# Three-branch attention with two heads' score and value products side by side, and one compressed-branch step for four heads

## The chip, the cores and the metric

The kernel runs on one core of one Trainium2 chip. The metric is the device time of one execution in microseconds (us), from three runs. The engines of the core work beside each other, each through its own queue in order: TensorE (products and transposes, which write PSUM), VectorE, ScalarE, GpSimd (POOL) and SyncE, which here issues DMAs.

## What is computed

Three blocks of a small transformer on 256 tokens of width 1024: retention with a mixture of experts, a three-branch attention with a mixture of experts, and a block of a state space model with a dilated attention and a feed-forward part. The change touches only the three-branch attention (the reference's `nsa_shared_kv` and `nsa_attention`): 16 query heads in 4 groups of 4, each group sharing its keys and values, head width 64. Each head attends to compressed keys (15 of them, pooled from windows of 32 tokens), to selected blocks, and to a window; the three results are weighted by gates and added. With 256 tokens every block of 64 is selected and every earlier token lies in the window, so both of these are causal attentions with different keys and values.

```python
        s = jnp.einsum('bgrqd,bgnd->bgrqn', qb, k_cmp).astype(jnp.float32)
        p_cmp = masked_softmax(s, cmp_end[None, :] <= t[:, None])
        o_cmp = jnp.einsum('bgrqn,bgnd->bgrqd', p_cmp.astype(dt), v_cmp)
...
        s = jnp.einsum('bgrqd,bgqkd->bgrqk', qb, ks).astype(jnp.float32)
        p = masked_softmax(s, (key_pos <= t[:, None])[:, :, None])
        o_slc = jnp.einsum('bgrqk,bgqkd->bgrqd', p.astype(dt), vs)
...
        s = jnp.einsum('bgrqd,bgkd->bgrqk', qb, kw).astype(jnp.float32)
        p = masked_softmax(s, wmask)
        o_win = jnp.einsum('bgrqk,bgkd->bgrqd', p.astype(dt), vw)
        o = gb[..., 0:1] * o_cmp + gb[..., 1:2] * o_slc + gb[..., 2:3] * o_win
```

## The kernel before

The whole network is one program; a planner (`schedule_with_timeline_sim=True`) orders each engine's instructions from the program text, its dependencies and its own estimate of times, so the order on an engine is not that of the text. `tc.issue_after(x)` holds the instructions inside it behind x in that order.

Products of full precision weights are made of three products of split operands (`mm3`, L237 to L241: L239, L240, L241); the split itself is a cast on ScalarE (L228) and a subtraction on VectorE (L230). Plain float32 products appear in the trace as two MATMUL records each, transposes as one.

The three-branch attention is `nsa` (from L955). It makes keys and values, then the compressed ones (L1077 to L1097): `kcz` holds compressed keys, `vcm` [16, 4, 64] compressed values with the 15 positions on partitions. `proj(I["w_q"], ...)` with `rope` makes the queries in two halves (L1100 to L1108), each of 8 heads: `qT` has two heads of 64 features on the 128 partitions. The first half serves groups 0 and 1.

Then come 8 steps over 4 groups g and 2 token tiles tb of 128 tokens. `scores(g, tb)` (L1113) makes, for the two head pairs pr of the group, the compressed scores of the pair (L1123, mask L1124), and for each head sl of the pair the scores over selected and window keys together (L1129; 64 partitions are contracted, [128, 2, S] results, S = 128 or 256 keys), then the causal mask, added by a bfloat16 product with the identity (L1130), the row maximum on VectorE (L1132) and two exponentials on ScalarE that also add up the denominators (L1134). The compressed scores have a maximum on VectorE (L1125) and an exponential per head (L1137). Denominators and gates make the factor `sc` (L1140 to L1142), and VectorE scales the probabilities (L1147); GpSimd scales the compressed ones (L1143).

`values(g, tb)` transposes the probabilities (L1161), copied from PSUM by VectorE and ScalarE in turn (L1163, L1165), and the compressed probabilities of the four heads, 16 columns each (L1169, L1171); then it adds all value products of a head half in one PSUM tile `po` (L1180): head half sl = 0 writes partitions 0 to 63, sl = 1 partitions 64 to 127. The result is split for the next projection (L234, L235). `scores` of the next step is asked for ahead of `values` of this one.

PSUM tiles of one bank come from three rings: `pmm` (4 banks: projections, scores and, here, compressed scores), `pat` (2: value results), `ptr` (2: transposes). The output projection (`w_no`, L1195 to L1198) takes all four banks of `pmm`; the planner runs its products between the last values. `ln_route` and the experts (`moe`) follow.

Of the kernel before, what the change touches and what calls it, by code (L numbers as in the profile page):

```python
# [20 lines left out]
EPS = 1e-5  # L21
# [4 lines left out]
OFFSET = 2.0 ** 20  # what tells the tokens of an expert from the others in their ranks  # L26
# [4 lines left out]
# where the first weights of a layer's experts go, in their order, and the order of loading where it is another one  # L31
# [4 lines left out]
# ---------------------------------------------------------------- host layout  # L36
# [137 lines left out]
# ---------------------------------------------------------------- kernel body  # L174
class Prog:
# [30 lines left out]
    # PSUM tiles of one bank  # L206
# [36 lines left out]
    def unit_a(self, outs, src, aT, k0, nk):  # L243
        """tokens on partitions: outs[t] [128, 512] += aT^T . unit (4 k tiles from k0 of nk)"""
# [10 lines left out]
    def ends_a(self, units, pool=()):  # L255
        """the last units of a projection, (outs, src, aT, k0, nk, tile of aT at k0): one token tile after the other;
        pool: what GpSimd's share of the splits comes after"""
# [15 lines left out]
    def unit_b(self, out, src, aT, k0, nk, engs=(None, None)):  # L273
        """features on partitions: out [128, 2, 256] += unit^T . aT (8 k tiles from k0 of nk)"""
# [8 lines left out]
    def unit_a256(self, outs, src, aT):  # L283
        """tokens on partitions: outs[t] [128, 256] = aT^T . unit (8 k tiles)"""
# [10 lines left out]
    def router(self, l, pool, room, tags, bufs):  # L295
        """the router's weights with the gain of the norm before it, and what its shift adds to the scores"""
# [16 lines left out]
    def route(self, t, pool):  # L313
        """the experts of token tile t: two of the best of four groups; the lower index first where equal"""
# [11 lines left out]
        # a group's score: the sum of its two best  # L326
# [8 lines left out]
        # how many of its group come before each one  # L335
# [12 lines left out]
        # the rank of each token within its expert, in order: OFFSET + rank where the expert is the token's  # L348
# [10 lines left out]
    def onehot(self, qd, t, r, pool):  # L359
        """which token of tile t has which slot of the experts 4 qd to 4 qd + 3 (r: the ranks)"""  # L360
# [7 lines left out]
    def ln_route(self, po, gb, hT, router, pool):  # L368
        """h = LN(alpha h + po), and each token's experts; hT [128, 2, 8, 128] is room"""
# [60 lines left out]
    def rstd(self, out, var):  # L430
        """out = (var + EPS) ** -0.5"""
# [6 lines left out]
    def ln_rows(self, i, gb):  # L438
        """gain and shift of norm i on all partitions, [128, 2, 1024]"""
        src = self.I["ln_r"][i]  # L440
        self.nc.gpsimd.dma_start(gb, bass.AP(tensor=src.tensor, offset=src.offset, ap=[[0, 128], [1024, 2], [1, 1024]]))
        return gb
# [1225 lines left out]
```

## Time and profile before

| what | value |
|---|---|
| median of 3 runs | 1499.23 us (1496.37 to 1500.24) |
| span of the profiled execution | 1498.9 us |
| TensorE busy | 1427.4 us, 95% of the span |
| VectorE busy | 776.1 us, 52% |
| ScalarE busy | 555.0 us, 37% |
| granted TensorE clock, mean | 0.978 of full speed |

The windows view gives for a stretch (from:to in us) its length and then the busy us of PE (TensorE products), PEld (its weight loads), DVE (VectorE), ACT (ScalarE) and POOL (GpSimd), each with its instruction count, then the granted clock, the DMA engines' busy share and GB/s. A timeline row gives start, busy us, engine, line, operation, written tile<-read tiles, for TensorE the rows*columns of the array in use and the moving shape, and the count of merged instructions; idle time before it stands in brackets. A group row gives line, engine, operation, tiles, shapes and count, then busy us and mean ns of one, then the engine's idle time before them and what ended it. Busy times of matmuls that follow one another overlap, so the distance between two starts tells what one costs.

### The profile page before, as it was taken

Reading aid. Unit: us, or ns where it says so; the run is one execution under the profiler, and the core shown is the slowest. Engines: PE = TensorE matmul, PEld = TensorE weight load, DVE = VectorE, ACT = ScalarE, POOL = GpSimd, SP = SyncE. Lnnn points to the kernel's source line nnn. Section 1 sums busy time; section 2 is a strip of 40 time slices with the busy share of each in tenths; the row PEclk is TensorE's granted clock in tenths of the full one; section 3 lists DMA queues with packets and bytes.
Section 4 is the critical chain, followed back from the end, with each engine's and each line's share of the span. In section 5 each row is a group of like instructions: output and inputs, shape, how many; then the busy total and the mean of one; then the engine's idle time right before and its main releaser. Section 6 shows DMA issues by size and latency. Waiting matters only on the chain. (4 is left out here: it accounts for less than half of the span.)

```text
span 1498.9 us, 20993 instructions
## 1 busy us (share of the span) xinstructions
PE 1427.4 (95%) x8363; PEld 1016.1 (68%) x8363; DVE 776.1 (52%) x1229; ACT 555.0 (37%) x978; POOL 232.8 (16%) x206
## 2 busy tenths in 40 slices
PE   7999988998998999989998999999999999899997
PEld 6888764443444875564443444997999999699986
DVE  5655563221215456553221215598999775745445
ACT  3434421110112555611110112566878554344442
POOL 2222121000002420021000001002443320211111
PEclk9999998999999999998998999999999999999999
DMA  9845677999984473166999984553765435545550
GB/s 359 330 155 169 257 279 280 375 417 389 414 351 166 160 273 145 57 255 263 362 419 389 414 319 177 198 207 112 265 211 196 156 127 171 194 144 194 187 179 28
DMA packets 64489, 365.16 MB, mean 244 GB/s; under 512 B 7472, under 2 KB 13120, under 8 KB 27648
## 3 DMA queue, kind: packets, MB, share of 16 engines
q1 hardware_dynamic: 60576, 348.75, 62.0%
q0 software_dynamic: 3808, 15.00, 2.8%
q8 instruction: 68, 1.11, 0.3%
q14 instruction: 37, 0.30, 0.1%
HBM read 362.53 MB, written 1.18 MB: 243 GB/s over the span
## 5 line engine op out<-in xcount | busy, mean ns | idle before, releaser
L230 DVE TENSOR_TENSOR wlo<-raw,whi 128x1024 fp32r<-128x1024 f32 x239 | 297.8, 1251 | 230.3 <-ACT whi L228 229.8
L228 ACT CAST whi<-raw 128x1024 fp32r<-128x1024 f32 x254 | 265.0, 1048 | 308.0 <-PE mm L241 129.9
L797 PE MATMUL mm<-raw,xg 128*64 128x512 f32 x744 | 187.2, 618 | 0.0
L241 PE MATMUL mm<-th,wlo 128*128 128x256 f32 x544 | 154.9, 285 | 4.3 <-DVE wlo L230 4.3
L239 PE MATMUL mm<-th,whi 128*128 128x256 f32 x544 | 155.9, 287 | 0.0
L240 PE MATMUL mm<-tl,whi 128*128 128x256 f32 x544 | 154.8, 285 | 0.0
L797 PEld LDWEIGHTS mm<-raw,xg 128*64 128x64 f32 x744 | 56.5, 141 | 93.2 <-issue 88.7
L241 PEld LDWEIGHTS mm<-th,wlo 128*128 128x128 f32 x544 | 104.2, 192 | 5.7 <-DVE wlo L230 4.7
L239 PEld LDWEIGHTS mm<-th,whi 128*128 128x128 f32 x544 | 104.3, 192 | 2.3 <-issue 1.2
L240 PEld LDWEIGHTS mm<-tl,whi 128*128 128x128 f32 x544 | 104.3, 192 | 1.3 <-issue 1.1
L235 DVE TENSOR_TENSOR y<-mm,y 128x512 fp32r<-128x512 f32 x32 | 22.0, 692 | 143.5 <-ACT y L234 142.3
L230 POOL TENSOR_TENSOR wlo<-raw,whi 128x1024 fp32r<-128x1024 f32 x15 | 37.5, 2505 | 305.7 <-ACT whi L228 305.7
L817 PE MATMUL mm<-raw,wk 128*64 128x512 f32 x344 | 80.5, 596 | 0.9 <-ACT wk L810 0.9
L240 PE MATMUL at<-tl,whi 128*128 128x256 f32 x264 | 74.8, 284 | 0.2 <-DVE tl L235 0.2
L239 PE MATMUL at<-th,whi 128*128 128x256 f32 x264 | 74.7, 283 | 0.2 <-ACT th L234 0.2
L241 PE MATMUL at<-th,wlo 128*128 128x256 f32 x264 | 74.7, 283 | 0.0
L234 ACT CAST y<-mm 128x512 fp32r<-128x512 f32 x32 | 18.7, 586 | 121.0 <-PE mm L817 120.8
L817 PEld LDWEIGHTS mm<-raw,wk 128*64 128x64 f32 x344 | 25.7, 137 | 45.7 <-issue 42.7
L850 DVE TENSOR_TENSOR h<-h,at 128x512 f32<-128x512 f32 x48 | 31.7, 685 | 46.4 <-PE at L844 45.0
L241 PE MATMUL mm<-whi,xl 128*128 128x512 f32 x128 | 51.2, 400 | 0.0
L240 PEld LDWEIGHTS at<-tl,whi 128*128 128x128 f32 x264 | 50.7, 192 | 0.7 <-DVE tl L235 0.4
L239 PEld LDWEIGHTS at<-th,whi 128*128 128x128 f32 x264 | 50.6, 192 | 0.7 <-ACT th L234 0.5
(448 smaller groups left out, 3152.9 us busy)
## 6 DMA issues: line engine op xcount, KB each, us to landing
raw<-in_w_moe SPq DMA_DIRECT2D x136, 1024.0 KB, 9.9
raw<-in_w_in SPq DMA_DIRECT2D x37, 1024.0 KB, 4.9
raw<-in_w_ret SPq DMA_DIRECT2D x31, 1024.0 KB, 5.0
wlo<-in_w_moe SPq DMA_DIRECT2D x40, 512.0 KB, 10.0
whi<-in_w_moe SPq DMA_DIRECT2D x40, 512.0 KB, 9.5
raw<-in_w_up SPq DMA_DIRECT2D x16, 1024.0 KB, 4.8
raw<-in_w_dn SPq DMA_DIRECT2D x16, 1024.0 KB, 4.9
hT<-in_w_moe SPq DMA_DIRECT2D x8, 1024.0 KB, 11.3
```

The source lines that it names most:

```text
L228: self.nc.scalar.copy(hi, src)
L230: (eng or self.nc.vector).tensor_sub(lo, src, hi.bitcast(F32))
L234: self.nc.scalar.copy(hi, src)
L235: self.last = self.nc.vector.tensor_sub(lo, src, hi.bitcast(F32))
L239: mm(out, lh, rh, start=start, stop=False)
L240: mm(out, lh, rl, start=False, stop=False)
L241: return mm(out, ll, rh, start=False, stop=stop)
L797: P.last_gu = nc.tensor.matmul(p[e * 64:(e + 1) * 64], xg[:, k, s0 + e * 64:s0 + e * 64 + 64], r[e][:, k2], start=k == 0, stop=k == 7)
L817: nc.tensor.matmul(pd[j][e * 64:(e + 1) * 64], hT_[:, k, e * 64:(e + 1) * 64], r[e][:, j], start=k == 0, stop=k == 3)
L850: V.tensor_add(h[:, t, c], h[:, t, c], p)
```

## The change

Scores: the compressed scores of all four heads of the group now come first, in a tile of the `pat` ring; one maximum, one subtraction, one exponential and one sum treat four heads at once, in two fixed tiles `Pcs` of 4 x 32 columns. For each head pair the two heads' score products are issued one behind the other, on partitions 0 to 63 and 64 to 127, into two banks, and both masks come after them. The first of a pair waits for the last exponential of the pair before last (`done[-2]`).

Values: the products of both head halves alternate. The compressed probabilities of four heads are transposed at once (128 columns); the compressed values `vcz` [128, 4, 4, 64] are kept once for each head position on 32 partitions of their own, with zeros elsewhere, so that a head's product runs over 128 rows and 128 moving columns. `hv` is the hidden layer spread out to 4 x 32 columns to make them.

Order: the second half of the queries is made after the first scores. The rest of the diff takes comments out of the text. Its core:

```diff
-        vcm = small.tile([16, 4, 64], F32, name="vcm", bufs=1)
+        vcz = small.tile([128, 4, 4, 64], F32, name="vcz", bufs=1)
+        Pcs = [small.tile([128, 4, 32], F32, name=f"Pc{i}", bufs=1) for i in range(2)]
...
-            G.memset(vcm, 0.0)
+            G.memset(vcz, 0.0)
+            for Pc in Pcs:
+                G.memset(Pc, 0.0)
...
-        p = P.pat([16, 4, 64])
+        hv = early.tile([128, 2, 4, 4, 32], F32, name="hv")
+        G.memset(hv, 0.0)
+        for hb in range(2):
+            V.tensor_copy(hv[:, hb, :, :, 0:15], hidT[:, hb, 1, :, None, 0:15].to_broadcast([128, 4, 4, 15]))
+        p = P.pat([128, 4, 64])
         for g in range(4):
             for hb in range(2):
-                mm(p[0:15, g], hidT[:, hb, 1, g, 0:15], wc2[:, 1, hb, 0:64], start=hb == 0, stop=hb == 1)
-        V.tensor_copy(vcm[0:15], p[0:15])
+                mm(p[:, g], hv[:, hb, g].rearrange("p r n -> p (r n)"), wc2[:, 1, hb, 0:64], start=hb == 0, stop=hb == 1)
+        for r in range(4):
+            V.tensor_copy(vcz[32 * r:32 * r + 32, r], p[32 * r:32 * r + 32])
         router = P.router(1, rp, early, ("rw", "lnp"), 1)
-        for c in range(2):
+        def queries(c):
...
-        heads.close()
-        oh = hT_pool.tile([128, 8, 256], F32R, tag="Th", name="oh")
-        ol = hT_pool.tile([128, 8, 256], F32R, tag="Tl", name="ol")
+        done = []
         def scores(g, tb):
             S = 128 * (tb + 1)
             ts = slice(tb * 128, tb * 128 + 128)
-            nm = small.tile([128, 2, 3, 2], F32, tag="nm", name="nm", bufs=2)
+            nm = small.tile([128, 2, 2, 2], F32, tag="nm", name="nm", bufs=2)
+            nmc = small.tile([128, 4], F32, tag="nmc", name="nmc", bufs=2)
             den = small.tile([128, 2, 3, 2], F32, tag="den", name="den", bufs=2)
             Pt = room(f"P{tb}", [128, 2, 2, 2, S])
-            Pc = small.tile([128, 2, 2, 16], F32, tag="Pc", name="Pc", bufs=2)
-            pc = P.pmm([128, 2, 2, 16])
+            Pc = Pcs[tb]
+            pc = P.pat([128, 2, 2, 16])
             for pr in range(2):
                 q = qT[:, 2 * g + pr, ts]
                 mm(pc[:, pr], q, kcz[:, g], start=True, stop=False)
                 mm(pc[:, pr], P.identb, cmb[:, tb, None, :].to_broadcast([128, 2, 16]), start=False, stop=True)
-                V.tensor_reduce(nm[:, pr, 0], pc[:, pr], axis=AX.X, op=ALU.max, negate=True)
+            pch = pc.rearrange("p a s n -> p (a s) n")
+            V.tensor_reduce(nmc, pch, axis=AX.X, op=ALU.max)
+            V.tensor_tensor(Pc[:, :, 0:16], pch, nmc[:, :, None].to_broadcast([128, 4, 16]), op=ALU.subtract)
+            A.activation(Pc[:, :, 0:16], Pc[:, :, 0:16], AF.Exp)
+            V.tensor_reduce(den[:, :, 0], Pc[:, :, 0:16].rearrange("p (a s) n -> p a s n", a=2), axis=AX.X, op=ALU.add)
+            for pr in range(2):
+                q = qT[:, 2 * g + pr, ts]
+                ps = [P.pmm([128, 2, 256]) for _ in range(2)]
+                pair = []
                 for sl in range(2):
                     c = slice(64 * sl, 64 * sl + 64)
-                    ps = P.pmm([128, 2, 256])
-                    mm(ps[:, :, 0:S], q[c], kz[c, g, :, 0:S], start=True, stop=False)
-                    mm(ps[:, :, ts], P.identb, P.causalb[:, None, :].to_broadcast([128, 2, 128]),
-                       start=False, stop=True)
-                    V.tensor_reduce(nm[:, pr, 1:3, sl], ps[:, :, 0:S], axis=AX.X, op=ALU.max, negate=True)
+                    with tc.issue_after(pair[0].ins) if pair else nullcontext():
+                        pair.append(mm(ps[sl][:, :, 0:S], q[c], kz[c, g, :, 0:S], start=True, stop=False))
+                if len(done) > 1:
+                    tc.add_manual_dep(pair[0].ins, done[-2].ins.name, mybir.DependencyInfo(
+                        mybir.DependencyClass.Sync, mybir.DependencyReason.ANTI), reason="both of a pair")
+                with tc.issue_after(pair[1].ins):
+                    for sl in range(2):
+                        mm(ps[sl][:, :, ts], P.identb, P.causalb[:, None, :].to_broadcast([128, 2, 128]),
+                           start=False, stop=True)
+                for sl in range(2):
+                    V.tensor_reduce(nm[:, pr, :, sl], ps[sl][:, :, 0:S], axis=AX.X, op=ALU.max, negate=True)
                     for br in range(2):
-                        A.activation(Pt[:, pr, br, sl], ps[:, br, 0:S], AF.Exp,
-                                     bias=nm[:, pr, 1 + br, sl:sl + 1], accum_out=den[:, pr, 1 + br, sl:sl + 1])
-                for sl in range(2):
-                    A.activation(Pc[:, pr, sl], pc[:, pr, sl], AF.Exp, bias=nm[:, pr, 0, sl:sl + 1],
-                                 accum_out=den[:, pr, 0, sl:sl + 1])
+                        last = A.activation(Pt[:, pr, br, sl], ps[sl][:, br, 0:S], AF.Exp,
+                                            bias=nm[:, pr, br, sl:sl + 1], accum_out=den[:, pr, 1 + br, sl:sl + 1])
+                done.append(last)
             sc = small.tile([128, 2, 3, 2], F32, tag="sc", name="sc", bufs=2)
             V.reciprocal(sc.rearrange("p a b c -> p (a b c)"), den.rearrange("p a b c -> p (a b c)"))
             V.tensor_mul(sc, sc, gat[:, tb, 12 * g:12 * g + 12].rearrange("p (a s b) -> p a b s", a=2, s=2))
             V.tensor_scalar(sc[:, :, 0], sc[:, :, 0], cmpc[:, 32 + tb:33 + tb], None, op0=ALU.mult)
-            G.tensor_tensor(Pc, Pc, sc[:, :, 0, :, None].to_broadcast([128, 2, 2, 16]), op=ALU.mult)
+            Pca = Pc[:, :, 0:16].rearrange("p (a s) n -> p a s n", a=2)
+            G.tensor_tensor(Pca, Pca, sc[:, :, 0, :, None].to_broadcast([128, 2, 2, 16]), op=ALU.mult)
...
-            p = P.ptr([16, 2, 2, 128])
-            for sl in range(2):
-                for pr in range(2):
-                    nc.tensor.transpose(p[:, sl, pr], Pc[:, pr, sl], P.ident)
-            PTc = rp.tile([16, 2, 2, 128], F32, tag="S", name="PTc", bufs=1)
+            p = P.ptr([128, 128])
+            nc.tensor.transpose(p, Pc.rearrange("p r n -> p (r n)"), P.ident)
+            PTc = rp.tile([128, 128], F32, tag="S", name="PTc", bufs=1)
             A.copy(PTc, p)
             po = P.pat([128, 2, 128])
-            jobs = []
-            for br in range(2):
-                for sb in range(nb):
-                    jobs.append((vv[:, sb, br, g], lambda sl, br=br, sb=sb: PT[:, sl, br, sb]))
-            jobs.append((vcm[:, g], lambda sl: PTc[:, sl]))
-            for sl in range(2):
-                for n, (lh, rh) in enumerate(jobs):
-                    mm(po[sl * 64:(sl + 1) * 64], lh, rh(sl), start=n == 0, stop=n == len(jobs) - 1)
+            for n, (br, sb) in enumerate((br, sb) for br in range(2) for sb in range(nb)):
+                for sl in range(2):
+                    mm(po[sl * 64:(sl + 1) * 64], vv[:, sb, br, g], PT[:, sl, br, sb], start=n == 0, stop=False)
+            for pr in range(2):
+                for sl in range(2):
+                    mm(po[sl * 64:(sl + 1) * 64, pr], vcz[:, 2 * pr + sl, g], PTc, start=False, stop=pr == 1)
             P.hilo(oh[:, 2 * g:2 * g + 2, ts], ol[:, 2 * g:2 * g + 2, ts], po)
 
         order = [(g, tb) for g in range(4) for tb in range(2)]
-        ahead = None
+        queries(0)
+        ahead = scores(0, 0)
+        queries(1)
+        heads.close()
+        oh = hT_pool.tile([128, 8, 256], F32R, tag="Th", name="oh")
+        ol = hT_pool.tile([128, 8, 256], F32R, tag="Tl", name="ol")
...
```

## Rows read from the trace of the kernel before

**Rows 1.** The profile's page: busy us, share of the span and instructions by engine.
```profile
PE 1427.4 (95%) x8363; PEld 1016.1 (68%) x8363; DVE 776.1 (52%) x1229; ACT 555.0 (37%) x978; POOL 232.8 (16%) x206
```

**Rows 2.** Windows view, the attention stretch: busy us by engine, clock, DMA, GB/s.
```profile
629.00:663.00 34.00, 34.00 (x157) 23.93 (x155) 15.62 (x31) 9.22 (x17) 1.46 (x3) 1.00 0.50 178
553.00:663.00 110.00, 109.43 (x509) 62.00 (x507) 61.76 (x175) 57.02 (x229) 7.61 (x14) 1.00 0.36 135
```

**Rows 3.** TensorE's timeline, scores of token tile 1: start, us, line, shapes, records.
```profile
576.24 1.12 PE L1129 MATMUL mm<-kz,qT 64*128 64x512 f32 x2
577.29 0.28 PE L1130 MATMUL mm<-causalb,identb 128*128 128x256 bf16 x1
577.50 1.12 PE L1129 MATMUL mm<-kz,qT 64*128 64x512 f32 x2
578.56 0.28 PE L1130 MATMUL mm<-causalb,identb 128*128 128x256 bf16 x1
578.68 0.60 PE L1161 MATMUL tr<-com,P 128*128 128x128 f32 x4
579.21 1.08 PE L1180 MATMUL at<-Q,vv 128*64 128x256 f32 x4
```

**Rows 4.** TensorE's timeline, scores of token tile 0.
```profile
588.67 0.70 PE L1129 MATMUL mm<-kz,qT 64*128 64x256 f32 x2
589.29 0.28 PE L1130 MATMUL mm<-causalb,identb 128*128 128x256 bf16 x1
589.51 0.70 PE L1129 MATMUL mm<-kz,qT 64*128 64x256 f32 x2
```

**Rows 5.** TensorE's timeline, value products and transposes of the compressed branch.
```profile
583.46 0.64 PE L1180 MATMUL at<-PTc,vcm 16*64 16x256 f32 x2
584.03 1.94 PE L1180 MATMUL at<-Q,vv 128*64 128x256 f32 x8
...
587.13 0.60 PE L1169 MATMUL tr<-com,Pc 128*16 128x128 f32 x4
587.66 1.08 PE L1180 MATMUL at<-Q,vv 128*64 128x256 f32 x4
```

**Rows 6.** TensorE's timeline, value products of the later dilated attention.
```profile
1021.16 1.95 PE L1248 MATMUL at<-dPT,v 128*64 128x256 f32 x16
```

**Rows 7.** VectorE's groups, 553 to 663: count, busy us, mean ns, idle before.
```profile
L1132 DVE TENSOR_REDUCE nm<-mm 128x2 f32<-128x512 f32 x16 | 11.0, 690 | 8.4 <-PE mm L1130 8.3
L1147 DVE TENSOR_SCALAR P<-P,sc 128x256 f32<-128x256 f32 x32 | 9.1, 355 | 0.0
...
L1147 DVE TENSOR_SCALAR P<-P,sc 128x128 f32<-128x128 f32 x32 | 6.8, 282 | 0.0
L1132 DVE TENSOR_REDUCE nm<-mm 128x2 f32<-128x256 f32 x16 | 6.6, 422 | 6.3 <-PE mm L1130 6.2
...
L1125 DVE TENSOR_REDUCE nm<-mm 128x2 f32<-128x32 f32 x16 | 2.9, 184 | 6.1 <-PE mm L1124 6.0
```

**Rows 8.** ScalarE's groups, 553 to 663.
```profile
L1134 ACT ACTIVATE P<-mm,nm 128x256 f32<-128x256 f32 x32 | 14.8, 471 | 8.7 <-PE tr L1161 5.6 <-DVE nm L1132 3.0
...
L1137 ACT ACTIVATE Pc<-mm,nm 128x16 f32<-128x16 f32 x32 | 8.3, 267 | 1.0 <-DVE nm L1125 1.0
```

**Rows 9.** Windows view of the later state space stage.
```profile
1050.00:1162.00 112.00, 109.30 (x958) 103.54 (x955) 103.84 (x162) 86.95 (x201) 43.82 (x33) 1.00 0.65 222
```

**Rows 10.** Timeline where the compressed keys and values are made.
```profile
536.58 0.55 PE L1089 MATMUL at<-hidT,wc 128*128 128x64 f32 x4
...
537.06 1.07 PE L1096 MATMUL at<-wc,hidT 128*15 128x64 f32 x16
...
538.92 0.74 POOL L1008 TENSOR_TENSOR qr<-rope,rope 128x256 f32<-128x256 f32 x1 [20.08 <-DVE rope L1000]
```

**Rows 11.** Windows view of the stretch behind the attention.
```profile
680.00:690.00 10.00, 8.69 (x33) 4.21 (x33) 4.67 (x20) 0.53 (x2) 2.39 (x3) 0.63 0.21 11
690.00:700.00 10.00, 10.00 (x54) 4.92 (x54) 1.38 (x2) 1.87 (x2) 0.00 (x0) 1.00 0.92 379
```

## Prediction

> **What bounds the kernel now.** I read the profile from the outside in. The page first: TensorE is busy 95% of the span, and no other engine is above 52%, PEld aside [rows 1]. That is an average over very different stages, so next comes the windows view of the stretch that the change touches, from the first score product of the attention (553 us) to the last product of its output projection (663 us): TensorE is busy 109.4 of 110.0 us at a granted clock of 1.00, its 2.4 GHz level, with VectorE at 61.8 and ScalarE at 57.0 [rows 2]. TensorE waits for nobody there: whatever is taken from its queue is taken from the time, until another engine is late. In the last 34 us, once the output projection's products fill the gaps, VectorE has 15.6 us of work; so the 76 us ahead of them hold 61.8 - 15.6 = 46.1 us of it [rows 2]. Third, TensorE's own timeline, where the distance from one start to the next is the price of a step (the busy times overlap). A float32 product shows as two records.
>
> **Score products.** Today each head's product is followed by its causal mask, and the next head's product comes only then. For token tile 1 (256 keys) two heads take 578.68 - 576.24 = 2.44 us: 1.05 for a product, 0.21 from the mask to the next product on 64 rows, 1.06 for the second product, 0.12 for a mask that is followed by work on 128 rows [rows 3]. For tile 0 (128 keys) it is 589.51 - 588.67 = 0.84 a head, 1.68 for two, 0.62 of each head being the product [rows 4]. The changed order is product, product, mask, mask. No row shows two products on disjoint row halves, so I bound it from both sides. If the partner is hidden wholly, a pair costs one product and two masks: 1.05 + 0.24 = 1.29 and 0.62 + 0.24 = 0.86, a gain of 1.15 and 0.82; with 8 pairs of each tile, 15.8 us. If the halves don't overlap, only the turns from mask to product go: 2.10 + 0.24 = 2.34 and 1.24 + 0.24 = 1.48, a gain of 0.10 and 0.20, 2.4 us in all. Below nothing it can't go by itself, as the instructions are the same. I take 15.0, near the upper end, because the nearest row, which pairs products on column halves, shows full overlap (next part); the 0.8 us are an allowance of mine for the partner's later start.
>
> The Trainium skill ("TensorE: Matmul & The Clock Gate", Part 3, measured speedup) gives 3.07 for four row tiles of an ideal 4; an estimate by the same share of ideal (1.54 for two) would leave about 10 of these 15 us. No row here shows it.
>
> **Value products.** Today all products of one head half stand in line, then all of the other. In the dilated attention the same form (128 rows, 64 columns, 256 moving) is issued half by half in turn, and sixteen records take 1.95 us there [rows 6], where eight take 1.94 us here [rows 5]: a pair on column halves costs what one costs. Now a half has 584.03 - 583.46 = 0.57 us for the compressed branch plus, for tile 0, 588.67 - 587.66 = 1.01 (its busy time of 1.08 reaches 0.07 into the next step), for tile 1 by the same cut 1.94 - 0.07 = 1.87 [rows 4, 5]: 3.16 and 4.88 us for both halves. After, the selected and window part costs 1.87 and 1.01 for both. The compressed part becomes four products of 128 moving columns on full rows: eight records, four pairs, each half as long as a pair of 256 columns (1.87 / 8 = 0.23), so 0.47. That makes 2.34 and 1.48, a gain of 2.54 and 1.68; with four groups 16.9 us.
>
> **Compressed branch.** Four transposes of 16 columns (587.66 - 587.13 = 0.53 [rows 5]) become one of 128; four such take 579.21 - 578.68 = 0.53 [rows 3], so 0.13: 0.40 less, times 8, 3.2 us. Its scores are as before on TensorE. ScalarE's 32 exponentials at 0.267 us [rows 8] become 8. VectorE gives two reductions of 0.184 a tile for two reductions and a subtraction over 64 elements, each between 0.184 and 0.422 [rows 7]; at 0.25 that is 0.4 us a tile more, 3 us in all (1.5 to 7). The wide compressed values need 128 weight columns instead of 15: four such records take 537.06 - 536.58 = 0.48, so sixteen 1.9, against 1.0 today [rows 10]: 0.9 us lost. VectorE's two copies and four copies ahead of it, at most 0.42 each, minus one, are 2.1 us; I cost them at nothing, since TensorE has projection products to run, and up to 2.1 where it doesn't. The larger memsets on GpSimd also cost nothing: it stands idle for 20 us ahead of the query rotation [rows 10].
>
> **What is moved.** The second half of the queries goes behind the first scores: its two weight loads on SP (which pass no other load), its splits, its rotation on VectorE and GpSimd, its transposes. TensorE then has those products to run while VectorE and ScalarE work on the first tile's softmax. Today there is next to no idle time at that spot to win [rows 2], so nothing is booked.
>
> **The added wait.** The first product of a pair waits for ScalarE's last exponential of the pair before last, which frees both banks at once. TensorE runs its queue in order, so transposes, value products and the next tile's scores stand behind it, and VectorE's reductions and copies wait for those. Two pairs may be in flight; see the last rival for its price.
>
> **The sum.** TensorE loses 15.0 + 16.9 + 3.2 - 0.9 = 34.2 us. Of this the last 34 us of the stretch lose one set of values of each tile, 2.54 + 1.68 + 0.80 = 5.0 us; TensorE stays the bound there. The 76 us ahead lose 30.1 and have 46 us left on TensorE, while VectorE has 46.1 + 3 = 49, of which the first tile's softmax (four reductions at 0.42, eight scalings at 6.8 / 32 = 0.21, 3.4 us [rows 7]) now runs beside the queries: 46. So the cover is used up: two engines with the same work, tied by a chain. In the state space stage VectorE is busy 103.8 of 112 us (93%) with TensorE busy as well [rows 9]; 46 / 0.93 = 49. Here the look-ahead is one tile and every pair goes TensorE, VectorE, ScalarE, so I take 84%: 55 us instead of 76. Gain 21 + 5 - 0.9 = 25 us. Does it survive? Behind the attention the DMA share falls to 0.21 before the expert layer starts and rises to 0.92 with it [rows 11]; its loads are released by its own progress, so the whole rest should move forward. The profiled execution spans 1498.9 us, the median is 1499.2: forecast 1474 us, 1468 to 1481.
>
> Against the change speaks the Trainium skill, "TensorEngine Tiling (Array Packing)", PSUM Bottleneck: packing speeds up the products and not the emptying of PSUM, which may become the limit. The trace agrees in kind: the score reductions alone are 11.0 + 6.6 = 17.6 us of VectorE [rows 7].
>
> **Rivals.** (1) TensorE stays the bound throughout: VectorE keeps up, all 34 us are won, 1465 us. For it: 93% in [rows 9]; against it: 46 us on both engines. (2) Row halves don't overlap: 12.6 us of the scores stay, TensorE needs 59 of the 76 us and binds again, some 60 with the chain: gain 16 + 5 - 1 = 20, 1479 us, to 1485 if the chain costs more. For it: no row shows such a pair; against it: column halves do overlap. (3) The order falls apart: the instruction order is planned, not that of the text, and transposes stand between score products today [rows 3]. If every pair is cut, 2.4 + 3.2 us are left, 1494 us. Against it: the sixteen records of [rows 6] stand together. (4) Slower: a new wait takes the place. If TensorE's queue puts nothing between a pair and its softmax, each pair costs its whole chain: 1.3 us of products, 0.69 of the first reduction, four exponentials at 0.47 [rows 7, 8], 3.9 us for tile 1; with tile 0 by half the reductions' and products' lengths about 2.8; eight of each are 54 us. With the 28 us of other TensorE work (46 less 18 of paired scores) that is 82 us for 76, and a transposed tile that waits for its copy likewise adds some 8: 14 - 5 + 1 = 10 us more, 1509 us. It decides once TensorE idles over 30 / 16 = 1.9 us a pair; at half of that a gain of 10 is left. Against it: one tile's values are there to be put between.
>
> **How the numbers follow.** A measurement of this kernel can tell about 0.3%, 4.5 us. Chances: forecast 0.55, rival (1) 0.12, (2) 0.17, (3) 0.04, (4) 0.07, and 0.05 for a stall that eats the gain to within 4.5 us. Faster: 0.55 + 0.12 + 0.17 + half of 0.04 = 0.86; the same 0.07; slower 0.07. The range reaches from rival (1) to beyond (2), 1463 to 1488, and leaves (3), (4) and the stall out, 0.16.
>
> **What would show it.** Right: score records of two heads starting within 0.1 us of each other; value records in pairs, 1.9 us for sixteen; the attention stretch some 25 us shorter with VectorE at 80 to 90% ahead of the projection; TensorE's idle time now ended by VectorE and ScalarE. Wrong: pairs 1 us apart (rival 2), other records between partners (3), TensorE idle at the score products until ScalarE's exponentials (4), or the expert layer starting earlier and ending as late as before.

## The result, and the profile after

The changed kernel takes 1479.29 us, median of 4 runs (1478.40 to 1481.21), beside 1499.74 us (1496.37 to 1500.73) for the kernel before on the same chip: ratio 0.9868 [0.9845, 0.9890], 20.5 us faster. The forecast was 25 us faster, 1474 (1468 to 1481, and 1463 to 1488 with its nearest rivals): the sign and the range hold, the size is 4.5 us too large. A second set of runs on another chip gives 0.9862 [0.9841, 0.9882] (`a0_changed_again` below). The profiled execution spans 1477.0 us.

Lines have moved: compressed scores L1133 (mask L1134), score products L1148, causal masks L1155, maxima L1158, exponentials L1160, scaling L1172, transposes L1186 (copies L1188, L1190), Pc transpose L1192, value products L1199, compressed value products L1202, query transposes L1116. First the page's engine line, then four windows of the attention stretch, with columns as in [rows 1, 2].

```profile
PE 1407.8 (95%) x8371; PEld 1012.1 (69%) x8371; DVE 775.1 (52%) x1242; ACT 546.5 (37%) x922; POOL 234.9 (16%) x209
```

The windows:

```profile
541.00:565.00 24.00, 21.98 (x99) 15.37 (x100) 15.67 (x35) 11.87 (x36) 7.05 (x7) 0.89 0.41 149
565.00:590.00 25.00, 24.81 (x167) 13.97 (x166) 19.62 (x69) 16.11 (x69) 1.21 (x4) 0.97 0.27 110
590.00:612.00 22.00, 22.00 (x143) 12.74 (x142) 16.77 (x58) 15.40 (x61) 0.79 (x3) 1.00 0.00 1
612.00:640.00 28.00, 28.00 (x162) 20.73 (x160) 14.30 (x27) 8.45 (x16) 1.47 (x3) 1.00 0.12 39
```

TensorE lost 19.6 us of busy time and is still the bound: from 565 on it is busy 24.81 of 25, 22.00 of 22 and 28.00 of 28 us. VectorE reaches 19.62 of 25 and 16.77 of 22, 77% of these 47 us. The clock column says 0.89 and 0.97 where it said 1.00 in the whole stretch before [rows 2].

TensorE's timeline now shows the pairs. The score products of tile 0 and tile 1, each row holding two products (x4) and two masks (x2):

```profile
568.60 0.70 PE L1148 MATMUL mm<-kz,qT 64*128 64x256 f32 x4
569.24 0.39 PE L1155 MATMUL mm<-causalb,identb 128*128 128x256 bf16 x2
569.56 0.86 PE L1199 MATMUL at<-Q,vv 128*64 128x256 f32 x5
...
571.59 1.13 PE L1148 MATMUL mm<-kz,qT 64*128 64x512 f32 x4
572.65 0.39 PE L1155 MATMUL mm<-causalb,identb 128*128 128x256 bf16 x2
572.88 1.04 PE L1186 MATMUL tr<-com,P 128*128 128x128 f32 x8
573.85 0.65 PE L1199 MATMUL at<-Q,vv 128*64 128x256 f32 x2
574.42 0.41 PE L1133 MATMUL at<-kcz,qT 128*128 128x32 f32 x2
...
576.85 1.08 PE L1199 MATMUL at<-Q,vv 128*64 128x256 f32 x6
577.86 0.33 PE L1192 MATMUL tr<-com,Pc 128*128 128x128 f32 x1
578.12 0.65 PE L1199 MATMUL at<-Q,vv 128*64 128x256 f32 x2
...
583.53 0.27 PE L1192 MATMUL tr<-com,Pc 128*128 128x128 f32 x1
583.74 1.08 PE L1199 MATMUL at<-Q,vv 128*64 128x256 f32 x8
584.75 0.41 PE L1133 MATMUL at<-kcz,qT 128*128 128x32 f32 x2
```

A pair of tile 1 takes 572.88 - 571.59 = 1.29 us where two heads took 2.44 [rows 3], a pair of tile 0 569.56 - 568.60 = 0.96 against 1.68 [rows 4]. The value products are half a success: the eight records at 583.74 are four products in two pairs, 1.01 us, but the two records at 573.85 are one product alone that costs 0.57, and the six at 576.85 are one pair and one product alone. Counting records that start within 0.04 us of their partner: 15 of 16 score pairs stand together, but only 15 of 24 pairs of value products and 12 of 16 of the compressed ones.

The list of what TensorE waited for between 535 and 643 us (line, releaser, total, times, longest) has grown; before there were two waits of 0.3 and 0.2 us.

```profile
PE tr L1116 <- POOL qr L1011: 0.8, 1, 0.8
PE mm L1148 <- DVE rope L1002: 0.8, 1, 0.8
PE at L1133 <- ACT qT L1117: 0.7, 1, 0.7
PE at L1199 <- DVE Q L1188: 0.2, 1, 0.2
```

The three large ones all hang on the queries, whose second half was moved. Two of them stand inside the one score pair that came apart (x2 instead of x4):

```profile
558.67 1.12 PE L1148 MATMUL mm<-kz,qT 64*128 64x512 f32 x2
560.59 0.65 PE L1116 MATMUL tr<-com,qr 128*128 128x128 f32 x4 [0.80 <-POOL qr L1011]
562.00 1.09 PE L1148 MATMUL mm<-kz,qT 64*128 64x512 f32 x2 [0.76 <-DVE rope L1002]
```

Around these waits the clock falls to its 1.2 GHz level (0.50) twice:

```profile
540.20:542.60 2.40, 1.71 (x15) 1.21 (x14) 2.05 (x5) 0.60 (x1) 1.78 (x2) 1.00 0.00 0
542.60:546.00 3.40, 3.40 (x15) 2.16 (x14) 1.70 (x6) 2.30 (x12) 0.44 (x1) 0.50 0.88 308
563.10:566.50 3.40, 3.40 (x14) 2.11 (x14) 1.37 (x3) 3.40 (x13) 0.34 (x1) 0.50 1.01 424
```

Summing the distances from start to start in TensorE's timeline, from the first product of the compressed hidden layer to the last of the output projection, gives the account (us; the last three columns are experiments below):

| step | before | after | e1 | e4 | e5 |
|---|---|---|---|---|---|
| score products | 26.90 | 15.73 | 14.26 | 17.12 | 22.72 |
| causal masks | 5.25 | 4.92 | 4.43 | 4.86 | 4.86 |
| value products | 23.61 | 16.24 | 16.75 | 12.90 | 14.69 |
| compressed values | 9.14 | 5.42 | 5.07 | 4.50 | 6.14 |
| Pc transposes | 4.24 | 1.78 | 1.78 | 1.76 | 1.71 |
| making of vcm / vcz | 1.00 | 1.76 | 1.76 | 1.76 | 1.76 |
| query transposes | 1.87 | 2.91 | 2.01 | 2.76 | 2.77 |
| TensorE idle | 0.57 | 2.43 | 1.89 | 3.22 | 2.22 |
| whole stretch | 126.1 | 107.6 | 104.1 | 105.0 | 113.1 |

The stretch is 18.5 us shorter. The rest of the span, 21.9 - 18.5 = 3.4 us, is an earlier start (536.6 to 535.1; over all kernels here it lies between 535.0 and 538.0) and 836.2 to 834.3 us behind the stretch. Of these 1.9 us, 1.2 are work of the router (L398, L407) that stood behind the output projection before and now stands between its last products, inside the stretch. Nothing was given back later.

### The profile page after: what moved, and what is told of

Same layout as the page of the kernel before. It is cut to its first block, busy times and chain, and to the rows that moved or that the text cites. A ratio compares the mean times of both kernels' runs of the same rounds, so it can differ in the third digit from the quotient of the medians.

```text
span 1477.0 us, 20923 instructions
## 1 busy us (share of the span) xinstructions
PE 1407.8 (95%) x8371; PEld 1012.1 (69%) x8371; DVE 775.1 (52%) x1242; ACT 546.5 (37%) x922; POOL 234.9 (16%) x209
## 5 line engine op out<-in xcount | busy, mean ns | idle before, releaser
L230 DVE TENSOR_TENSOR wlo<-raw,whi 128x1024 fp32r<-128x1024 f32 x239 | 297.4, 1248 | 223.4 <-ACT whi L228 222.9
L241 PEld LDWEIGHTS mm<-th,wlo 128*128 128x128 f32 x544 | 104.1, 191 | 5.6 <-DVE wlo L230 4.7
L230 POOL TENSOR_TENSOR wlo<-raw,whi 128x1024 fp32r<-128x1024 f32 x15 | 37.4, 2501 | 301.3 <-ACT whi L228 301.3
L844 PE MATMUL at<-y,ST 128*128 128x512 f32 x112 | 38.5, 430 | 13.3 <-PEq L856 12.3
```

The costliest lines, as they stand in the source:

```text
L230: (eng or self.nc.vector).tensor_sub(lo, src, hi.bitcast(F32))
L241: return mm(out, ll, rh, start=False, stop=stop)
L844: nc.tensor.matmul(p, ST[:, t * 128:(t + 1) * 128], y[:, j, n], start=n == 0, stop=n == 1)
```

## Experiments

Theory A: TensorE stays the bound, so what counts is how many partners really stand side by side in its queue and how long it idles or runs at the low clock around the queries. Theory B, the forecast's: once TensorE has lost its work, VectorE limits the loop. The ratios are to the kernel before, run on the same chip; 0.9862 to 0.9868 is the changed kernel.

**The changed kernel again**, beside e5 to e7, with no edit.

> The changed kernel as it is, beside the other kernels of this comparison and on their chip: 1478 to 1482 us by every theory.

1479.87 us, 0.9862 [0.9841, 0.9882]. Both half-clock stretches of 3.4 us and the same waits are there: they belong to the kernel and not to one execution.

**Score products one head after the other**, without pairs and without the added wait; all else as changed.

```diff
-                ps = [P.pmm([128, 2, 256]) for _ in range(2)]
...
+                    ps = P.pmm([128, 2, 256])
+                    mm(ps[:, :, 0:S], q[c], kz[c, g, :, 0:S], start=True, stop=False)
+                    mm(ps[:, :, ts], P.identb, P.causalb[:, None, :].to_broadcast([128, 2, 128]),
+                       start=False, stop=True)
```

> The changed kernel with product, mask, product, mask for the two heads, without the added wait; all else as changed. Theory A: the 11.5 us that score products and masks lost on TensorE come back: 1489 to 1493 us. Theory B, VectorE's chain sets the pace: less than 6 us come back, 1480 to 1485 us. Where the wait costs anything by itself, the result lies lower by that.

1492.33 us, 0.9947 [0.9928, 0.9966]: 12 us above the changed kernel. Score products take 28.89 us, 13.2 more than after, idle time falls to 0.76. Pairing the scores is thus the largest part of the gain, as theory A had it. (Ten us of this kernel's stretch ran at half clock, against 6.8 in the changed one, and its projection products take 1.7 us more, so a little of the 12 is the clock.)

**Value products half by half.**

```diff
-            for n, (br, sb) in enumerate((br, sb) for br in range(2) for sb in range(nb)):
-                for sl in range(2):
+            for sl in range(2):
+                for n, (br, sb) in enumerate((br, sb) for br in range(2) for sb in range(nb)):
...
-            for pr in range(2):
-                for sl in range(2):
+                for pr in range(2):
```

> The changed kernel with the value products of one head half in line and then the other's, as before the change (the wide compressed products stay, two by two of a half). Theory A, TensorE is the bound: the 7.4 us that the selected and window products lost on TensorE come back, and some 2 us of the paired compressed products: 1486 to 1491 us. Theory B, TensorE has slack because VectorE's chain sets the pace: less than 4 us come back, 1479 to 1483 us.

1486.87 us, 0.9917 [0.9897, 0.9937], some 7 us above. Values take 20.89 and compressed values 6.69 us, 5.9 more together, and idle time is 0.75 us longer: theory A again.

**Without the added wait** on `done[-2]`.

```diff
-                if len(done) > 1:
-                    tc.add_manual_dep(pair[0].ins, done[-2].ins.name, mybir.DependencyInfo(
-                        mybir.DependencyClass.Sync, mybir.DependencyReason.ANTI), reason="both of a pair")
```

> The changed kernel without the added wait of the first of a pair for the last exponential of the pair before last; each product still waits for its own bank. Theory A, the wait holds pairs together: without it the planner issues a first product as soon as its own bank is free, other records come between the partners, and part of the 11.5 us of the score products is lost: 3 to 8 us slower than the changed kernel, 1483 to 1488 us. Theory C (rival 4 of the prediction in small), the wait holds TensorE's queue up: 1 to 4 us faster, 1476 to 1479 us.

1483.19 us, 0.9884 [0.9867, 0.9900]: 3.3 us slower than the changed kernel of the same batch. TensorE's timeline shows why:

```profile
571.71 1.12 PE L1148 MATMUL mm<-kz,qT 64*128 64x512 f32 x2
572.76 0.66 PE L1199 MATMUL at<-PTc,vcz 128*64 128x128 f32 x8
573.35 0.65 PE L1183 MATMUL tr<-com,P 128*128 128x128 f32 x4
573.93 1.12 PE L1148 MATMUL mm<-kz,qT 64*128 64x512 f32 x2
574.99 0.39 PE L1152 MATMUL mm<-causalb,identb 128*128 128x256 bf16 x2
```

One product of a pair (x2), other work for 1.17 us, then its partner. Only 7 of 16 pairs are left and the score products take 22.72 us. A single product costs 572.76 - 571.71 = 1.05 us, the price of two in the changed kernel. The wait, in the forecast only a danger, is what keeps most partners together. By the code, without it the first product is free to go as soon as one bank is, and the second may not be; the trace shows the partners apart, not which bank the second waited for.

**VectorE relieved.** The 64 scalings of the probabilities are left out (so the selected and window parts enter unnormalised); they were 15.9 us of VectorE.

```diff
-                        V.tensor_scalar(Pt[:, pr, br, sl], Pt[:, pr, br, sl], sc[:, pr, 1 + br, sl:sl + 1], None,
-                                        op0=ALU.mult)
```

> The changed kernel without the 64 scalings of the probabilities by denominator and gate: that part of the computation is left out, 16 us of VectorE's work, and one link of each tile's chain. Theory A, TensorE is the bound with 2.4 us of idle time in the stretch: at most 3 us faster, 1476 to 1480 us. Theory B, VectorE sets the pace: 8 us or more faster, below 1472 us.

1476.18 us, 0.9834 [0.9817, 0.9852]: 3.7 us below the changed kernel, for 16 us less on VectorE. The windows:

```profile
565.00:590.00 25.00, 25.00 (x167) 14.27 (x165) 15.04 (x46) 18.59 (x79) 2.19 (x6) 0.93 0.37 156
590.00:612.00 22.00, 22.00 (x155) 13.52 (x154) 12.73 (x38) 15.61 (x62) 0.89 (x3) 1.00 0.00 1
```

TensorE is busy in all 47 us with VectorE at 27.8 (59%). Of the 3.7 us, 2.1 are value products (16.24 to 14.12): 18 of 24 pairs stand together instead of 15, which fits probabilities that are ready sooner. Theory B falls: VectorE's 16 us are worth 3.7 at most, and as a limit of its own it is worth little here.

**Values in the order in which they become ready.** The probabilities are transposed with the head half innermost, so that two partners' blocks lie in the same PSUM tile and come with the same copy. The scalings follow that order.

```diff
-            PT = room(f"Q{tb}", [128, 2, 2, nb, 2, 128])
+            PT = room(f"Q{tb}", [128, 2, nb, 2, 2, 128])
...
-            blocks = [(sl, br, sb, pr) for sl in range(2) for br in range(2) for sb in range(nb) for pr in range(2)]
+            blocks = [(sl, br, sb, pr) for br in range(2) for sb in range(nb) for sl in range(2) for pr in range(2)]
...
-                    mm(po[sl * 64:(sl + 1) * 64], vv[:, sb, br, g], PT[:, sl, br, sb], start=n == 0, stop=False)
+                    mm(po[sl * 64:(sl + 1) * 64], vv[:, sb, br, g], PT[:, br, sb, sl], start=n == 0, stop=False)
```

> The changed kernel with the transposed probabilities kept by branch and key block first and by head half second, and scaled and transposed in that order, so that both halves of a value pair become ready with one copy; nothing is added or left out. In the changed kernel the halves become ready with different copies and the planner runs part of the products alone: 96 records cost 16.2 us where 48 pairs would cost 11.5. Theory A (TensorE is the bound, and pairs that fall apart are what the value term missed): 3 to 6 us faster, 1473 to 1476 us, and value records in pairs throughout. Theory B (VectorE's chain sets the pace): no change, 1478 to 1481 us.

1476.42 us, 0.9842 [0.9822, 0.9862], 3 to 4 us below the changed kernel. All 24 pairs of values and all 16 compressed ones stand together:

```profile
576.91 0.65 PE L1199 MATMUL at<-Q,vv 128*64 128x256 f32 x4
577.50 0.41 PE L1133 MATMUL at<-kcz,qT 128*128 128x32 f32 x2
...
579.43 0.65 PE L1199 MATMUL at<-Q,vv 128*64 128x256 f32 x4
580.83 0.65 PE L1199 MATMUL at<-Q,vv 128*64 128x256 f32 x4 [0.75 <-DVE Q L1188]
```

A pair by itself (x4) costs 577.50 - 576.91 = 0.59, about what the lone product at 573.85 cost after (0.57). Values and compressed values fall by 4.3 us. Of that 1.4 goes to score products (two pairs apart instead of one) and 0.8 to idle time.

**Queries first.** Both halves of the queries ahead of the first scores, as before the change.

```diff
         queries(0)
-        ahead = scores(0, 0)
         queries(1)
+        ahead = None
```

> The changed kernel (1479.3 us) with both halves of the queries made ahead of the first scores, as before the change; all else as changed. Theory A, TensorE stays the bound: the trace of the changed kernel shows TensorE idle for about 2.4 us and its clock at half for two times 3.4 us around the moved queries, so undoing the move should give 0 to 5 us back: 1474 to 1479 us. Theory B, the forecast's: VectorE's softmax of the first tile was hidden beside the moved queries, 3.4 us that show again: 1480 to 1484 us.

1477.08 us, 0.9857 [0.9833, 0.9881]. The interval overlaps that of the changed kernel, so the times alone don't tell the two apart; the time lies in theory A's range, and the profiles differ: the stretch is 3.5 us shorter, none of it at half clock, with score products 1.5, query transposes 0.9 and idle time 0.5 us less. By the profile, the move that was booked at nothing costs about that.

**Both: ready order and queries first.**

> Both halves of a value pair made ready with one copy, and both halves of the queries ahead of the first scores. Theory A: the two gains measured one by one (about 4 us each beside the changed kernel) come from different places, TensorE's value records and its clock, and add up: 7 to 9 us faster than the changed kernel, 1471 to 1474 us. Theory B, the one makes the other's slack: no more than 5 us, 1475 us or above.

1474.41 us, 0.9820 [0.9802, 0.9839]: 5.5 us below the changed kernel of the same batch, between the two theories. The times of e1 and e4 are too uncertain to say whether the two gains add up (their ratios alone give a sum of 4 to 6 us); by the profiles they don't quite, since the stretch is 4.4 us shorter and not 3.5 + 2.6 = 6.1. TensorE's timeline in e1, at the third of the four sets of query transposes:

```profile
556.51 0.66 PE L1116 MATMUL tr<-com,qr 128*128 128x128 f32 x4 [1.03 <-POOL qr L1011]
558.55 1.13 PE L1148 MATMUL mm<-kz,qT 64*128 64x512 f32 x4 [0.30 <-ACT P L1160]
```

and the window behind it:

```profile
557.20:564.00 6.80, 6.20 (x31) 2.91 (x32) 5.68 (x22) 5.97 (x25) 1.79 (x3) 1.00 0.97 396
```

The same two views of this kernel, the timeline first:

```profile
557.21 0.85 PE L1116 MATMUL tr<-com,qr 128*128 128x128 f32 x4 [1.03 <-POOL qr L1011]
559.68 2.08 PE L1148 MATMUL mm<-kz,qT 64*128 64x512 f32 x4
```

and the window:

```profile
557.50:564.30 6.80, 6.80 (x22) 2.80 (x20) 4.75 (x17) 4.44 (x21) 1.79 (x3) 0.50 1.00 382
```

The same wait of 1.03 us for the same releaser, behind nearly the same work; in e1 the clock stays at 1.00, here it is 0.50 for 6.8 us, and the pair at 559.68 takes 2.0 us instead of 1.07. Score products cost 17.40 us against 14.26. Of these 3.1 us, 1.06 is a second pair apart, as in e4 too; the other 2 are three score rows that run at half clock behind the wait, wholly or in part, and they are more than the 1.7 us that are missing from the sum.

**Work to keep the clock up.** A product of no use ahead of each set of four query transposes: in the changed kernel, in the ready order (e4), and in e7.

```diff
                 p = P.ptr([128, 4, 128])
+                mm(p[:, 0:2], P.ident, qr[:, 0, 0:1].to_broadcast([128, 256]), start=True, stop=True)
```

> The changed kernel with a product of no use (256 columns) ahead of each set of four query transposes, so that TensorE has work where it stands idle around the moved queries; it adds about 4 x 0.43 us of TensorE work. If the half-clock stretches cost the time there (two of 3.4 us, in which products take nearly twice as long, so some 3 us): they are gone, and the kernel is 1 to 3 us faster than the changed one. If the idle time itself is the loss and the clock only a by-product: no change, or up to 2 us slower.

> The kernel with values laid out in the order in which partners become ready, and the same products of no use ahead of the query transposes. If the clock costs what the half-clock stretches last by: 1 to 3 us below the kernel with the ready order alone (which stood 3.5 us below the changed one). If not: level with it or up to 2 us above.

> Ready order, both halves of the queries ahead of the first scores, and the products of no use. If the half-clock stretch of 6.8 us is what kept the two edits from adding up (7 to 9 us wanted, 5.5 measured): it vanishes, and the time is 2 to 3 us below the kernel without these products, 8 us below the changed one. If not: level with it or up to 2 us above.

e9 took 1483.55 us, 0.9882 [0.9860, 0.9905], 2 to 4 us above the changed kernel: a miss. e10 took 1477.26, 0.9850 [0.9829, 0.9871], level with e4 or 1 us above: the hoped-for gain is missed, and the time is that of the other branch. e11 took 1472.89, 0.9821 [0.9800, 0.9842], 1.5 us below e7 by the medians and level with it by the ratios, short of the 2 to 3 us. The timeline of e9:

```profile
542.65 0.68 PE L1115 MATMUL tr<-qr,com 128*128 128x256 f32 x2
543.17 0.60 PE L1117 MATMUL tr<-com,qr 128*128 128x128 f32 x4
544.92 0.96 PE L1115 MATMUL tr<-qr,com 128*128 128x256 f32 x2 [1.16 <-POOL qr L1010]
```

and its window:

```profile
541.00:565.00 24.00, 22.84 (x105) 17.38 (x103) 12.39 (x32) 9.21 (x25) 3.21 (x5) 0.79 0.17 54
```

The test was badly built: the added product reads `qr`, so at 544.92 it stands waiting 1.16 us for the first of the two rotation steps (L1010) that the transposes need as well, and fills no idle time. e9 then ran 10.2 us at half clock, with projection products at 0.43 us each instead of 0.23, and paid 2.4 us for the added products. e10 ran 3.4 us at half clock instead of 6.8 and saved 2.0 us of score products (1.06 of them because one pair more stands together), but paid 2.45. In e11 one of the added products does stand where the gap was:

```profile
555.37 0.70 PE L1115 MATMUL tr<-qr,com 128*128 128x256 f32 x2
556.47 0.66 PE L1117 MATMUL tr<-com,qr 128*128 128x128 f32 x4 [0.40 <-POOL qr L1011]
```

and the window behind it:

```profile
557.20:564.00 6.80, 6.80 (x36) 3.56 (x37) 6.23 (x22) 6.21 (x25) 1.81 (x3) 1.00 0.94 395
```

No half clock is left in its stretch. Against e7 score products fall by 2.2, query transposes by 0.6 and idle time by 0.6 us, the added products take 2.1: the stretch is 1.1 us shorter, and the two ratios can't be told apart. In both kernels 14 of 16 score pairs stand together, so this is the clock and the gap: the low clock costs real time, and buying it off costs nearly as much.

**The compressed branch narrow.** The changed kernel with `vcm`, four transposes of 16 columns and products over 16 rows as before, but the two halves in turn.

```diff
-            p = P.ptr([128, 128])
-            nc.tensor.transpose(p, Pc.rearrange("p r n -> p (r n)"), P.ident)
+            p = P.ptr([16, 2, 2, 128])
+            for sl in range(2):
+                for pr in range(2):
+                    nc.tensor.transpose(p[:, sl, pr], Pc[:, 2 * pr + sl, 0:16], P.ident)
...
-            for pr in range(2):
-                for sl in range(2):
-                    mm(po[sl * 64:(sl + 1) * 64, pr], vcz[:, 2 * pr + sl, g], PTc, start=False, stop=pr == 1)
+            for sl in range(2):
+                mm(po[sl * 64:(sl + 1) * 64], vcm[:, g], PTc[:, sl], start=False, stop=True)
```

> The changed kernel with the compressed branch as it was before the change: narrow compressed values, four transposes of 16 columns a tile, products of 256 columns on 16 rows, its two halves in turn so that they can overlap. TensorE bound: the transposes return (+2.5 us), the making of the wide values goes (-0.8), the products are as long paired as the four wide ones (within 0.5): 1 to 3 us slower than the changed kernel, 1480 to 1483 on its scale. Rival, the wide form as a whole brings what the compressed lines of TensorE fell by (3.7 + 2.5 - 0.8 = 5.4 us): 1485 or more.

1481.06 us, 0.9873 [0.9852, 0.9895]: not told apart from the changed kernel. On TensorE the transposes take 4.23 us (2.45 more), the making 1.00 (0.76 less), the products 4.63 (0.79 less): 0.9 us in all. So of the 3.7 us by which the compressed products fell, the wide layout brought none; alternating the halves brings them in the narrow layout as well (all its pairs stand together, and 4.63 us is near the 4.50 of e4, where all wide pairs do). The rival of 1485 or more is out. The profiled execution was the longest of its five: its stretch is 1.0 us shorter than after, with one half-clock stretch instead of two, but 838.7 us follow it where 834.3 did; why is left open.

## Why the prediction was right, step by step

**TensorE's bound before the change, and the survival of the gain: right.** The later stages moved forward and gave nothing back. **Row halves overlap: right**, and fully: a pair of tile 1 came out at the forecast 1.29 us. The estimate that scaled a figure for four row tiles of the Trainium skill ("TensorE: Matmul & The Clock Gate", Part 3) down to two, and left about 10 of the 15 us (redone with the prediction's prices, some 11), isn't borne out: 1.06 us for two products against 1.05 for one. Four tiles are in no run here. That settles rival (2).

**Score term: mis-sized, 15.0 forecast, 11.5 measured** (scores and masks, 32.15 to 20.65). Of the 3.5 us, one pair that the planner cut costs 1.06 (its second product waited for a bank that the projection of the moved queries still held), two pairs at half clock 2 x 0.52 = 1.04, and masks 1.1 more than the 16 x 0.24 forecast, part of it again at half clock. The allowance of 0.8 was meant for a late partner, which starts only 0.007 us later; it is used up by the kernel before, whose scores and masks sum to 32.15 where three rows had priced them at 33.0.

**Value term: mis-sized, 16.9 forecast, 11.1 measured** (32.75 to 21.66). This is the step that failed most. The price of a pair was right inside a run of pairs (1.01 for two at 583.74), but a pair by itself costs 0.59 and not 0.47. That all would be pairs was taken from the dilated attention [rows 6], whose probabilities are all there when the products are issued (their last copy ends at 1018.5 us, the products start at 1021.2). Here the copies arrive one by one, head half by head half, and the planner runs whichever product has its tile: 9 of 24 pairs fell apart. That was rival (3) in part, argued away by the wrong row. e4 confirms it: same products, partners ready together, 17.4 us, 4.3 of the 5.8 that are missing; the rest is that pairs cost more than priced, those by themselves and the compressed ones (0.28 us each in e4 for 0.23).

**Small terms.** Pc transposes 2.5 for 3.2, making of the wide values -0.8 for -0.9, both near. The four terms of the forecast come to 24.3 us for 34.2. Not in it: compressed scores were to stay and took 0.6 us more with their masks, query transposes 1.0, transposes of the probabilities 0.65, the output projection 0.4. That leaves 21.6 us less work on TensorE; with the 1.2 us of router work that moved in, the stretch is busy 20.4 us less.

**VectorE as a second limit: over-sized.** The forecast took 84% instead of full cover and gave away 55 - 46 = 9 us. This is a step that was wrong in its mechanism. Measured, TensorE idles 1.9 us more than before, nearly all at the queries; from 565 to 612 us it idles 0.2. The step set VectorE's 46 us against a TensorE with 46 us left; TensorE kept 14 us more than that, so the two never met; VectorE was busy 77% and not the 80 to 90% of the forecast. Hence e6's small gain. The rule that was cited against the change, the PSUM Bottleneck of the Trainium skill's "TensorEngine Tiling (Array Packing)", did not decide here: none of TensorE's four waits in the stretch was for the emptying of a bank that the packed products had filled.

**The moved queries: booked at nothing, cost some 3.5 us** by e1's profile, 1 to 4 by its times (idle time at the waits for `qr`, `rope` and `qT`, and about 3 us at the low clock). The forecast named the cover, projection products. At 541.5 us TensorE waits for ScalarE's copy of the first queries (L1117) while these products still lie behind the scores in its queue (the first starts at 545.5); at 560.6 and 562.0 they are used up. The wait at 560.6 ends with the second of GpSimd's two rotation steps, which took 1.55 and 1.70 us there, beside splits on VectorE (L230), and 0.73 us each for the next tile; whether the splits slowed them, no run tests.

So 34.2 - 9.1 = 25.1 was the difference of two terms that were both too large, and 20.4 - 1.9 = 18.5, with the earlier start and the shorter rest, is what came. That the two errors, 13.8 us and 7.2, went against each other is luck, and it kept the number near. The mechanism, TensorE bound to the end, was rival (1)'s; its size was near rival (2)'s 20 us; the forecast landed between for a reason that was partly wrong. **The added wait**, rival (4), never cost anything that shows: no row of the changed kernel's waits list names ScalarE's exponentials, and without it the kernel is 3.3 us slower. (In e1, e2, e4, e7, e8 and e11 score products do wait for an exponential, 0.2 to 0.8 us at a time.)

**The best version** is e7 or, with the added products, e11: 0.982 of the kernel before, some 6 us below the changed kernel.

## What to carry to other kernels

Side by side on the array is worth its full price only where both partners are ready together: give them one tile, one copy, one release, and check in the timeline that records stand in pairs, before counting the gain for all. Where a planner orders the queue, a dependency that holds the first partner back until the second can follow may pay for itself. And a bound engine's small gaps can cost more than their length, when the clock falls behind them, as it did behind some here and not behind others.

## What the runs showed of the hardware that was not expected

Two float32 products on the two row halves, into two banks, start 0.007 us apart and take 1.06 us, as one alone does. The granted clock of the attention stretch fell to 0.50 in ten of the fourteen profiled executions between 542 and 546 us, each time behind a gap of TensorE of 0.69 to 1.16 us and a row of narrow products (router, query transposes), and stayed up there in the four without such a gap at that place (before, e1, e7, e11). The gap alone doesn't decide: 1.03 us behind nearly the same work left the clock up in e1 and not in e7, 0.69 us was followed by 3.4 us in most kernels and by 10.2 in e3, and gaps of 0.76 us at 566 and 569 us in e9 and e10 by none. What else decides stays open.
